# Gate and up: where the residual waits, and a second place for raw weights

## The chip, the cores and the metric

The kernel runs on one core of a Trainium2 chip: TensorE (PE) multiplies, VectorE (DVE), ScalarE (ACT) and GpSimd (POOL) do the work between, SyncE (SP) issues nearly all DMAs. The metric is device time in microseconds, the median of several runs. The profile comes from one further execution.

## The reference, cut to what matters

Two layers act on 1152 tokens (1024 of a prompt, 8 x 16 of samples) with 1024 features. Each layer has a mixer and then a feed-forward part, and the change touches the latter alone:

```python
x = x + mix
x = x + swiglu(rmsnorm(x, p['norm_ffn'][layer]), p['ffn_w_gate'][layer],
               p['ffn_w_up'][layer], p['ffn_w_down'][layer])
```

So silu(h @ w_gate) * (h @ w_up) is formed for 2816 hidden features and multiplied by w_down; all in float32.

## The kernel before, in words

Activations lie as [feature on 128 partitions, tokens on the free axis]. x, the residual, is held in four SBUF tiles x0 to x3 of [128, 2, 1152]: two chunks of 128 features each. A dense product is three float32r matmuls of 384 columns: each operand is split into a rounded part (`whi` for weights) and its remainder (`wlo`), and high x high, high x low and low x high are added in PSUM (`mm3`, L434 to L438).

`ffn` has two stages, gate and up and then down. **Gate and up** runs over 22 tiles of 128 hidden features. For a tile f, SP loads the raw gate weights and the raw up weights, 512 KB each (`raws`, L633). The 24 products of four quarters of the features with three blocks of tokens, for gate and for up, are made of 20 products, as in a fast matrix product: their left operands are sums or differences of quarters of the weights (UP_A, L409), their right operands sums of blocks of activations, which are made once. Each product is 2 chunks x 3 matmuls. The 20 are handled in five panels of four products. For a panel, `weights` (L502)
- forms the sums on POOL (L518) into one of three buffers `cm`. Most sums have 256 columns, and two pairs are done together with 512; two panels have two sums each and take two quarters straight from the raw weights,
- rounds them on ScalarE (L522) into one of three places for split panels,
- takes the remainder on VectorE (L523).

Places and `cm` buffers are passed round. One place and two of the `cm` buffers lie where x2 and x3 were, since x has been turned into the operands by then; so in the trace they are called x, as in "x<-raw" (a sum) or "pa<-u,x" (a matmul). The residual was stored to DRAM (`d_r`) by the stage before.

`tile_of` (L526) orders the products of a tile and the sums of them. ScalarE copies some from PSUM (L549), VectorE adds and subtracts (L555), POOL does one subtraction (also L555), ScalarE applies SiLU (L608), POOL multiplies gate by up (L609), and SP stores the outcome to DRAM (`d_g`, L610), three stores a tile. The room for these is 15 temporaries of 384 columns, handed back after the stores.

The first two tiles are done while the operands are still being made. After them x0 and x1 are free; before the change the residual's first half is loaded there at once (L715 to L717), and tiles 2 to 21 follow in one loop (L724). Their raw weights all go to the same two buffers (L274), one for gate and one for up, so the load for tile f+1 waits until the last panel of tile f has been summed and split. x2 and x3 come back after the loop (L728 to L730), then the down product begins.

Each engine executes its own instructions in one fixed order, which the framework's scheduler sets at build time: by readiness in its own account of the time and by priority, where a priority is the order of the source and `Sooner` moves instructions to the front. Waits are semaphores at the tiles' first and last uses. All loads and stores of this stage go through SP's queue in order.

Of the kernel before, what the change touches and what calls it, by code (L numbers as in the profile page):

```python
"""Hybrid S5 / gated-DeltaNet / sliding-window encoder step on one core.

Activations are held as [feature on partitions, token on the free axis]; the 1024 prompt tokens come
first, then the 8 x 16 sample tokens. A dense product is three float32r passes over operands split
exactly into a rounded part and its remainder."""
# [23 lines left out]
T = TP + NS * LS  # L29
# [15 lines left out]
def ksplit(w):  # L45
    """[K, M] -> [M/128, 128 (k in its chunk), K/128 * 128] panels."""
    k, m = w.shape
    return np.ascontiguousarray(w.reshape(k // 128, 128, m // 128, 128).transpose(2, 1, 0, 3).reshape(m // 128, 128, k))


def halves(w):
    """[1024, 1024] -> [K halves, M/256, 128, 2 * 512] panels."""
    return np.ascontiguousarray(ksplit(w).reshape(4, 2, 128, 2, 512).transpose(3, 0, 2, 1, 4).reshape(2, 4, 128, 1024))


def cols(v):
    """[n * 128] -> [128, n]."""
    return np.ascontiguousarray(v.reshape(-1, 128).T)


def head_order():
    """Column order of q: row halves of a 128-tile hold a head of an even and of an odd kv group."""
    o = []
    for pair in range(2):
        for i in range(4):
            for par in range(2):
                h = 4 * (2 * pair + par) + i
                o += list(range(64 * h, 64 * h + 64))
    return np.array(o)


def s5_order():
    """Order of the S5 channels inside each 128: (channel of a group, group)."""
    return np.arange(512).reshape(4, 8, 16).transpose(0, 2, 1).reshape(512)


def layout(a):
    """The kernel's inputs: moved, copied and zero-padded only."""
# [52 lines left out]
def constants():  # L131
    """Depend on shapes alone."""
# [55 lines left out]
class Chunks:  # L188
    """Chunks of features in tiles of two: x[:, chunk, tokens]."""
# [4 lines left out]
    def new(self, i, shape, dt=F32):  # L194
        """A tile in the place of the i-th."""
# [7 lines left out]
def body(tc, nc, I, O):  # L203
# [19 lines left out]
    def mphase(**tags):  # L223
        """Five banks for the parts between the dense products: one ring, or one for each of the named tiles."""
# [25 lines left out]
    def behind(i, *others):  # L250
        """Queue an instruction behind others of its engine."""
# [4 lines left out]
    def log_tables(*others):  # L256
        """One load of the tables that Ln and Exp share, behind other activations."""
        return behind(S.preload_act_table_set("natural_log_exp_and_others"), *others)

    class Sooner:  # L260
        """Instructions inside go before others that are ready, as if traced n instructions earlier."""
# [16 lines left out]
    def parts(raw, pool=None, bufs=2):  # L278
        """Rounded part and remainder of a panel of weights."""
# [11 lines left out]
    def slots(name):  # L291
        """Per token block, the rounded part and the remainder of 4 + 4 chunks of features."""
# [24 lines left out]
    def sums(sq, w, tag=None):  # L317
        """Sum over partitions of sq, on all partitions (a bank)."""
# [11 lines left out]
    def square_in(x, k, b, i, new, parts, keep=None):  # L330
        """Squares of a chunk into partial sums over chunks; the partial sums with the last chunk.

        One running sum by GpSimd (and one by VectorE), and the last chunk's squares on their own."""
# [15 lines left out]
    def rms(r, b, parts, first=0):  # L349
        """1 / sqrt(mean of squares + eps) of a block's tokens, on all partitions, from parts of the sums of squares."""  # L350
# [18 lines left out]
    def norm(w, h, r, new, first, keep=None):  # L369
        """What fills the scales and, where there are, the operands of a norm as chunk k of block b of x, its i-th, is final."""  # L370
# [24 lines left out]
    # ------------------------------------------------------------------ feed-forward  # L395
    # Gate and up of three blocks of tokens t: with a_0 .. a_3 the gate's and a_4 .. a_7 the up's weights of a quarter q of the
    # features, and b_qt the activations, the 24 products are made of twenty, UP_A[i] times UP_B[i], UP_B in terms of
    # e0 = b_00 + b_01 + b_02 and e1 = b_10 + b_11 + b_12:
    #  0: (a6 - a7) b22                       1: a2 (e1 + b20 + b21 + b30)        2: (a7 - a0) (e0 - b31)
    #  3: -(a2 + a6) (b20 + b22)              4: -(a2 - a3) b30                   5: a0 (b00 + b01 + b12 - b31)  # L400
    #  6: (a6 - a5) b21                       7: (a4 + a7) e0                     8: (a2 - a1) e1
    #  9: -(a0 + a3) b31                     10: -(a4 + a5) b00                  11: -a7 (e0 - b22 - b31 - b32)
    # 12: -(a2 + a5) (e1 + b21)              13: (a5 - a0) (b00 + b12)           14: (a2 + a7) (b22 - b30)
    # 15: a5 (b00 + b11 + b12 + b21)         16: -(a1 + a5) (b10 + b12)          17: -(a0 + a4) (b00 + b02)
    # 18: (a3 + a7) (b30 + b32)              19: -(a0 + a1) b12
    # gate_0 = z + 1 + 4 + 19 - v            gate_1 = v + 5 - z - 8 - 9          gate_2 = 14 + 18 - 4 - 19 - s
    # up_0 = -(0 + 10 + 3 + 14) - z - 1      up_1 = 15 - y - 2 - 5 + 6 + 7       up_2 = y + 0 + 10 + s
    # with z = 12 + 15, v = 13 + 16, y = 13 - P17 and s = 2 + 5 + P11, each number the product of that number.
# [5 lines left out]
    # Down: the first block of tokens is multiplied plainly. For the other two, the four products of halves  # L414
    # C[i][j] = A[i][0] B[0][j] + A[i][1] B[1][j] are made of seven:
    # S1 = A21 + A22, S2 = S1 - A11, S3 = A11 - A21, S4 = A12 - S2,
    # T1 = B12 - B11, T2 = B22 - T1, T3 = B22 - B12, T4 = B21 - T2.
    # Panels of weights give A11 and A12, A21 and A22, S1 and S2, S3 and S4.
    PANELS = (("B11", "B21"), (None, "T4"), ("T1", "T2"), ("T3", "B22"))

    def left(raw, s12):
        """Sums of halves of two raw panels; the last two in place of the first panel, so once that is split."""
# [17 lines left out]
    def reserve(pool):  # L440
        """Place for split panels at the bottom of a pool."""
# [3 lines left out]
    def ffn(x, pre, l, w, nxt):  # L445
# [3 lines left out]
        # gate and up  # L449
# [37 lines left out]
        # sums of weights, split panels, and what the products make  # L487
# [14 lines left out]
        def weights(raw, ps, place=place):  # L502
            """Rounded parts and remainders of the left operands of up to four products."""
# [22 lines left out]
        def tile_of(f, raw, room, order, panels, early=False):  # L526
            """The products of a tile of f: those without the last block of tokens, then the others."""
# [9 lines left out]
            def prods(p, *ps, more=False):  # L537
                """Products into p; more of them, added to what has been read already."""
# [126 lines left out]
        # the first two tiles of f, while the operands of the twenty are made  # L665
# [48 lines left out]
        # x comes back; until then half of its place is for more panels  # L714
        for i in range(2):  # L715
            x.tiles[i] = x.new(i, [128, 2, T])
            Q.dma_start(x.tiles[i], d_r[i])  # L717
        t, u = x.new(2, [128, 2 * T], F32R), x.new(3, [128, 2 * T])
        extra += [[t[:, blk(i, 1024)] for i in range(2)], None, None]
        cms += [u[:, blk(i, 1024)] for i in range(2)]  # L720
        room = rooms[0] + [r[:, blk(UP_T[1])]]
        for t in (some("b13", 1), some(), some()):
            room += [t[:, c] for c in range(2)]
        for f in range(2, NF):  # L724
            last = f == NF - 1
            order = UP_ORDER[16:] + UP_ORDER[:16] if last else UP_ORDER
            finishing(tile_of(f, raws(f), room, order, [(order[i:i + 4],) for i in range(0, 20, 4)], last))
# [6 lines left out]
        # down, by pairs of tiles of f; the products of two pairs go to sums of the seven over all pairs  # L734
# [17 lines left out]
        def load(f):  # L752
            """A tile of f, and room for another block."""
# [12 lines left out]
        def right(ps, last):  # L766
            """Right operands of two pairs, and places for those of the pair that is multiplied plainly."""
# [28 lines left out]
        def into(terms, m, o, first=False):  # L796
            """The products of the terms, tile m of their columns, added to o."""
# [10 lines left out]
        # the last pair is multiplied plainly, and what it gives added with products of the seven that make the same part of x  # L808
        also = {"B21": (0, 1), "T4": (4, 1), "B22": (0, 2)}
        for j in range(0, len(pairs) - 1, 2):  # L810
# [24 lines left out]
            for q in range(4):  # L835
# [5 lines left out]
                for e, n in enumerate(PANELS[q]):  # L841
                    for m in range(4):
# [6 lines left out]
                        if last:  # L849
                            # the sums of the seven make x  # L850
# [26 lines left out]
    # ------------------------------------------------------------------ layer 0  # L877
# [98 lines left out]
    # b and a rows: beta, cumulative log decay and what follows from it  # L976
# [26 lines left out]
    def gate_in(hh, zz):  # L1003
        """The gate of a head."""
# [8 lines left out]
    # S5: u, chunk operators, and the states after each chunk  # L1013
# [11 lines left out]
    # powers 1 to 16 of the step over a chunk  # L1025
# [32 lines left out]
    # prompt: scans inside 8 groups of 16 chunks, then over the groups' ends, then what each group starts with  # L1058
# [27 lines left out]
    # convolutions, and what of the delta rule needs no recurrence  # L1086
# [35 lines left out]
    def l2norms(ys, tables):  # L1122
        """Scale pairs (y, scratch, log of a factor) to unit length of every token."""
# [60 lines left out]
    # inverses of the delta rule's triangular systems' blocks: 32 tokens, one block to a partition  # L1184
# [29 lines left out]
    # S5 outputs  # L1214
# [28 lines left out]
    # v  # L1243
# [25 lines left out]
    # S5: operands of the GLU  # L1269
# [16 lines left out]
    # delta rule, recurrence over 128-token tiles  # L1286
# [13 lines left out]
    def solved(TT, kg, vt, t, uu, wt, tag):  # L1300
        """u and w of a tile from the transposed inverse of its system."""
# [675 lines left out]
```

## Time and profile before

| | |
|---|---|
| median of 3 runs | 2831.28 us (2830.82 to 2835.2) |
| profiled execution: span | 2835.9 us (no other time of it is recorded) |
| TensorE clock granted, mean | 0.953 of full |
| busy: PE, DVE, ACT, POOL | 92%, 70%, 39%, 58% |
| loads of raw gate and up weights | 44 + 44 of 512 KB |
| loads of the residual (x<-d_r) | 8 of 1152 KB |

"Busy" is the share of the span in which an engine had an instruction running; matmuls overlap in the records, so the spacing of their starts tells more than their lengths. An engine's idle time is put down to what ended it, its releaser. In the rows further down a time in brackets is such an idle time.

### The profile page before, as it was taken

How to read it: one execution, taken by the hardware profiler on the slowest of the kernel's cores; microseconds unless marked ns; L12 is line 12 of the kernel's file. 1: busy time of each engine (PE TensorE's matmuls, PEld its weight loads, DVE VectorE, ACT ScalarE, POOL GpSimd, SP SyncE). 2: the span in 40 equal slices, each digit the busy share in tenths (PEclk: the TensorE clock that was granted, in tenths of full speed). 3: DMA queues.
4: the chain of work that ended last, by engine and by line, in shares of the span. 5: the costliest groups of instructions: out<-in, count | busy, mean ns of one | idle time of the engine just before them, and what ended most of it. 6: DMA issues, size and time to landing. Idle time of an engine off the chain costs nothing.

```text
span 2835.9 us, 40158 instructions
## 1 busy us (share of the span) xinstructions
PE 2618.7 (92%) x14777; PEld 2422.3 (85%) x14777; DVE 1977.8 (70%) x3195; ACT 1103.2 (39%) x2232; POOL 1639.5 (58%) x1659
## 2 busy tenths in 40 slices
PE   7898999998799999989999999998799999989996
PEld 6787898897799899989999966668789999979996
DVE  7757855568876666698866245557877666688977
ACT  4233574443433333343333144433333333344332
POOL 8659332225687777788532012114587777788744
PEclk9999999998899999989999999898899999989998
DMA  6523376531122222243213100202022222243311
GB/s 199 155 74 98 107 248 205 180 121 66 56 94 70 70 70 70 70 161 120 91 43 108 59 16 23 89 29 97 32 92 78 75 71 71 70 144 106 110 62 67
DMA packets 164165, 267.20 MB, mean 94 GB/s; under 512 B 34189, under 2 KB 123949, under 8 KB 162929
## 3 DMA queue, kind: packets, MB, share of 16 engines
q1 hardware_dynamic: 163392, 262.28, 28.8%
q8 instruction: 116, 1.90, 0.3%
q10 hardware_dynamic: 576, 2.36, 0.2%
q14 instruction: 81, 0.66, 0.1%
HBM read 186.92 MB, written 79.51 MB: 94 GB/s over the span
## 4 chain that ended last, share of the span: by engine, by line
PE 45%; POOL 22%; DVE 17%; DMA 7%; issue 5%; ACT 3%; SPq 1%; DVEq 0%; ACTq 0%; POOLq 0%
POOL x L518 8%; POOL cm L518 5%; PE pd L436 4%; PE pd L437 4%; PE pd L438 4%; DMA raw<-in_wu_dram 3%; PE pg L307 3%; PE pg L308 3%; PE pg L309 3%; DVE wlo L523 3%; PE pO L1889 2%; DMA raw<-in_wg_dram 2%; PE pg L1514 2%; PE pS L1862 2%; PE pg L1516 2%
## 5 line engine op out<-in xcount | busy, mean ns | idle before, releaser
L518 POOL TENSOR_TENSOR x<-raw 128x256 f32<-128x256 f32 (+1 forms) x372 | 353.1, 976 | 99.0 <-DMA raw<-in_wg_dram 85.5
L436 PE MATMUL pa<-u,whi 128*128 128x384 f32 x928 | 324.8, 350 | 41.4 <-DVE bt L555 14.3
L438 PE MATMUL pa<-u,wlo 128*128 128x384 f32 x928 | 311.2, 345 | 13.7 <-DVE wlo L523 13.7
L437 PE MATMUL pa<-u,whi 128*128 128x384 f32 x928 | 319.2, 344 | 1.7 <-DVE u L469 1.5
L518 POOL TENSOR_TENSOR cm<-raw 128x256 f32<-128x256 f32 (+1 forms) x244 | 236.2, 990 | 78.4 <-DVE wlo L523 28.0
L436 PE MATMUL pd<-g,whi 128*128 128x384 f32 x708 | 240.4, 340 | 0.9 <-DVE bt L555 0.9
L437 PE MATMUL pd<-g,whi 128*128 128x384 f32 x708 | 241.1, 341 | 0.0
L438 PE MATMUL pd<-g,wlo 128*128 128x384 f32 x708 | 238.2, 338 | 0.0
L436 PEld LDWEIGHTS pa<-u,whi 128*128 128x128 f32 x928 | 180.7, 195 | 55.6 <-DVE bt L555 15.9
L523 DVE TENSOR_TENSOR wlo<-x,whi 128x1024 fp32r<-128x1024 f32 (+1 forms) x132 | 155.4, 1177 | 101.7 <-ACT whi L522 101.3
L1850 POOL TENSOR_SCALAR p<-p,rd 128x192 f32<-128x192 f32 (+3 forms) x80 | 59.1, 741 | 287.4 <-DVE rd L1844 175.5
L522 ACT CAST whi<-x 128x1024 fp32r<-128x1024 f32 (+1 forms) x132 | 115.7, 876 | 236.8 <-POOL x L518 209.6
L438 PEld LDWEIGHTS pa<-u,wlo 128*128 128x128 f32 x928 | 179.2, 194 | 17.3 <-DVE wlo L523 17.3
L284 ACT CAST whi<-raw 128x1024 fp32r<-128x1024 f32 x113 | 116.3, 1049 | 178.1 <-PE pg L308 83.0
L437 PEld LDWEIGHTS pa<-u,whi 128*128 128x128 f32 x928 | 180.5, 195 | 3.4 <-DVE u L469 2.3
L436 PE MATMUL pa<-u,x 128*128 128x384 f32 x428 | 150.6, 352 | 31.0 <-ACT x L522 26.8
L285 DVE TENSOR_TENSOR wlo<-raw,whi 128x1024 fp32r<-128x1024 f32 x113 | 162.4, 1438 | 22.3 <-ACT whi L284 22.1
L437 PE MATMUL pa<-u,x 128*128 128x384 f32 x428 | 148.9, 348 | 0.0
L307 PE MATMUL pg<-h0h,whi 128*128 128x384 f32 x384 | 136.6, 356 | 12.4 <-DVE ut L941 11.4
L438 PE MATMUL pa<-u,x 128*128 128x384 f32 x428 | 143.9, 345 | 0.0
L764 DVE TENSOR_TENSOR g<-gf,g 128x384 fp32r<-128x384 f32 x132 | 136.7, 1062 | 5.8 <-ACT g L763 5.8
L436 PEld LDWEIGHTS pd<-g,whi 128*128 128x128 f32 x708 | 133.9, 189 | 1.7 <-DVE bt L555 1.6
(727 smaller groups left out, 7946.2 us busy)
## 6 DMA issues: line engine op xcount, KB each, us to landing
gf<-d_g SPq DMA_DIRECT2D x44, 576.0 KB
raw<-in_wg_dram SPq DMA_DIRECT2D x44, 512.0 KB
raw<-in_wu_dram SPq DMA_DIRECT2D x44, 512.0 KB
raw<-in_wd_dram SPq DMA_DIRECT2D x44, 512.0 KB
raw<-in_win_dram SPq DMA_DIRECT2D x21, 512.0 KB
d_r<-x SPq DMA_DIRECT2D x24, 384.0 KB
x<-d_r SPq DMA_DIRECT2D x8, 1152.0 KB
d_aq<-AQ SPq DMA_DIRECT2D x12, 576.0 KB
```

The source lines that it names most:

```text
L284: S.copy(hi, raw)
L285: V.tensor_sub(lo, raw, hi)
L307: PE.matmul(p[:, :BW], hi[:, c], rh, start=(i == 0), stop=False)
L308: PE.matmul(p[:, :BW], hi[:, c], rl, start=False, stop=False)
L309: PE.matmul(p[:, :BW], lo[:, c], rh, start=False, stop=(i == len(ks) - 1))
L436: PE.matmul(p, hi[:, c], uh, start=start, stop=False, skip_group_check=more)
L437: PE.matmul(p, hi[:, c], ul, start=False, stop=False, skip_group_check=more)
L438: PE.matmul(p, lo[:, c], uh, start=False, stop=stop, skip_group_check=more)
L518: (P.tensor_add if sg > 0 else P.tensor_sub)(cm[:, 256 * j:256 * (j + n)], fa, ga)
L522: S.copy(hi[:, c], src)
L523: V.tensor_sub(lo[:, c], src, hi[:, c])
L764: eng.tensor_sub(op[1], t, op[0])
```

## The change

The two tiles x0 and x1 are no longer filled with the residual after tile 1 of the features. Their room is taken as `back`. Tiles 3, 5, .. 17 load their raw weights into the two halves of the first of them; the even tiles and tiles 19 to 21 use the two buffers as before. When the loop reaches tile 19, the residual's first half is loaded into `back`. The changed file also has its comments and docstrings blanked, with the same line numbers up to the change.

```diff
-        # x comes back; until then half of its place is for more panels
-        for i in range(2):
-            x.tiles[i] = x.new(i, [128, 2, T])
-            Q.dma_start(x.tiles[i], d_r[i])
...
         t, u = x.new(2, [128, 2 * T], F32R), x.new(3, [128, 2 * T])
         extra += [[t[:, blk(i, 1024)] for i in range(2)], None, None]
         cms += [u[:, blk(i, 1024)] for i in range(2)]
+        back = [x.new(k, [128, 2 * T]) for k in range(2)]
         room = rooms[0] + [r[:, blk(UP_T[1])]]
         for t in (some("b13", 1), some(), some()):
             room += [t[:, c] for c in range(2)]
         for f in range(2, NF):
             last = f == NF - 1
+            if f == NF - 3:
+                for i in range(2):
+                    x.tiles[i] = back[i].rearrange("p (k t) -> p k t", k=2)
+                    Q.dma_start(x.tiles[i], d_r[i])
             order = UP_ORDER[16:] + UP_ORDER[:16] if last else UP_ORDER
-            finishing(tile_of(f, raws(f), room, order, [(order[i:i + 4],) for i in range(0, 20, 4)], last))
+            if f % 2 and f < NF - 3:
+                raw = [back[0][:, blk(i, 1024)] for i in range(2)]
+                for n, t in zip("gu", raw):
+                    Q.dma_start(t, I[f"w{n}{l}"][f])
+            else:
+                raw = raws(f)
+            finishing(tile_of(f, raw, room, order, [(order[i:i + 4],) for i in range(0, 20, 4)], last))
         for i in range(2, 4):
             x.tiles[i] = x.new(i, [128, 2, T])
             Q.dma_start(x.tiles[i], d_r[i])
```

## Rows read from the trace of the kernel before

**Rows 1.** The page: the chain that ended last, by engine and by line.
```profile
PE 45%; POOL 22%; DVE 17%; DMA 7%; issue 5%; ACT 3%; SPq 1%; DVEq 0%; ACTq 0%; POOLq 0%
POOL x L518 8%; POOL cm L518 5%; PE pd L436 4%; PE pd L437 4%; PE pd L438 4%; DMA raw<-in_wu_dram 3%; PE pg L307 3%; PE pg L308 3%; PE pg L309 3%; DVE wlo L523 3%; PE pO L1889 2%; DMA raw<-in_wg_dram 2%; PE pg L1514 2%; PE pS L1862 2%; PE pg L1516 2%
```
**Rows 2.** Windows, cut by TensorE's matmuls: tiles 4 to 18, both layers; tiles 6, 7.
```profile
core 0: us, PE busy (x) PEld busy (x) DVE busy (x) ACT busy (x) POOL busy (x), PEclk, DMA share, GB/s
811.20:1162.00 350.80, 326.42 (x1801) 318.79 (x1800) 236.12 (x361) 129.37 (x242) 268.56 (x274) 0.98 0.22 71
2115.60:2466.00 350.40, 327.81 (x1802) 320.05 (x1801) 236.96 (x361) 129.36 (x242) 269.33 (x273) 0.98 0.22 71
855.90:881.80 25.90, 22.81 (x122) 22.49 (x121) 17.13 (x26) 9.51 (x18) 18.75 (x21) 0.93 0.20 64
881.80:903.20 21.40, 21.19 (x122) 20.87 (x121) 14.38 (x23) 8.77 (x15) 17.17 (x19) 1.00 0.24 77
```
**Rows 3.** Timeline, TensorE, tile 6: start, duration, line, operation, idle before.
```profile
858.74 0.33 PE L437 MATMUL pa<-u,whi 128*128 128x384 f32 x1
...
859.95 0.34 PE L438 MATMUL pa<-u,wlo 128*128 128x384 f32 x1
863.38 0.61 PE L436 MATMUL pa<-u,x 128*128 128x384 f32 x1 [3.09 <-ACT x L522]
863.78 0.53 PE L437 MATMUL pa<-u,x 128*128 128x384 f32 x1
...
866.66 0.46 PE L437 MATMUL pa<-u,whi 128*128 128x384 f32 x1
```
**Rows 4.** Waits of TensorE, 844.48 to 1194.54: us, times, longest.
```profile
PE pa L436 <- ACT x L522: 13.4, 5, 3.1
PE pa L436 <- ACT whi L522: 2.2, 2, 1.3
PE b L438 <- DVE wlo L523: 1.7, 3, 0.8
```
**Rows 5.** The chain, 840 to 920: start, duration, what.
```profile
844.48 3.65 DMA raw<-in_wg_dram
...
857.28 0.98 POOL bt L555
...
861.87 0.52 ACT b L608
```
**Rows 6.** POOL's groups, 844.48 to 1194.54: busy, mean ns, idle before, releaser.
```profile
L518 POOL TENSOR_TENSOR x<-raw 128x256 f32<-128x256 f32 (+1 forms) x140 | 131.8, 968 | 36.0 <-DMA raw<-in_wg_dram 31.7 <-DMA raw<-in_wu_dram 4.3
L518 POOL TENSOR_TENSOR cm<-raw 128x256 f32<-128x256 f32 (+1 forms) x70 | 65.4, 956 | 16.4 <-DMA raw<-in_wg_dram 10.5 <-DMA raw<-in_wu_dram 5.9
```
**Rows 7.** Timeline, POOL and VectorE: sums, L555, L609 and a remainder.
```profile
781.25 0.75 POOL L518 TENSOR_TENSOR x<-raw 128x256 f32<-128x256 f32 x1 [4.01 <-DMA raw<-in_wg_dram]
...
848.20 0.73 POOL L518 TENSOR_TENSOR x<-raw 128x256 f32<-128x256 f32 x1 [4.18 <-DMA raw<-in_wg_dram]
...
857.24 1.00 POOL L555 TENSOR_TENSOR bt<-nt,bt 128x384 f32<-128x384 f32 x1
...
859.94 1.15 POOL L609 TENSOR_TENSOR b<-b,bt 128x384 f32<-128x384 f32 x1 [1.69 <-ACT b L608]
860.15 1.22 DVE L523 TENSOR_TENSOR wlo<-raw,whi 128x256 fp32r<-128x256 f32 x1
...
878.85 1.29 POOL L518 TENSOR_TENSOR cm<-raw 128x512 f32<-128x512 f32 x1
```
**Rows 8.** Timeline, SP: the loads of tile 3, of x0, and of tile 6.
```profile
773.64 0.38 SPq L717 DMA_DIRECT2D x<-d_r  x1
775.25 0.33 SPq L275 DMA_DIRECT2D raw<-in_wg_dram  x1
...
777.27 0.33 SPq L275 DMA_DIRECT2D raw<-in_wu_dram  x1
...
844.48 0.36 SPq L275 DMA_DIRECT2D raw<-in_wg_dram  x1
```
**Rows 9.** Line L523, 844.48 to 1194.54: ns shortest/median/longest, first and last start, forms.
```profile
L523 DVE TENSOR_TENSOR wlo<-x,whi x50: 677/1213/1366, 845.2 to 1188.9; 128x1024 fp32r<-128x1024 f32 x30, 128x512 fp32r<-128x512 f32 x20
L523 DVE TENSOR_TENSOR x<-raw,x x20: 411/590/782, 883.2 to 1194.3; 128x256 fp32r<-128x256 f32 x20
```

## The prediction

> **What bounds the kernel now.** First the chain that ended last: 22% of it is POOL, and by line the sums of weights (L518) lead with 8% and 5%, with the loads of raw weights behind them at 3% and 2% [rows 1]. All of these lie in gate and up, so the question is what one tile of features costs there. The windows cut at the first matmul of tiles 4 and 19 hold fifteen tiles each: 350.80 us in layer 0, 350.40 in layer 1, 23.37 a tile [rows 2]. A tile is 20 products of 6 matmuls, 120 matmuls. Undisturbed they start 0.173 us apart (eight starts from 858.74 to 859.95), so TensorE needs 120 x 0.174 = 20.9 us; 2.5 us a tile are lost. Tile 7 took 21.40 and tile 6 before it 25.90 [rows 2]: the loss is uneven, and falls mainly on every third tile.
>
> What it is made of: in tile 6 TensorE stops at 859.95 and goes on at 863.38, then starts matmuls 0.32 us apart from 863.78 to 866.66 (ten starts), which is the 1.2 GHz level; ahead of that it had been idle [rows 3]. So an idle of 3 us costs nearly 1.5 us more at the low clock. In fifteen tiles TensorE waits 13.4 us for casts of ScalarE into the third place for panels (five times, up to 3.1), the largest entry by far [rows 4]. The chain says why that cast was late: 3.65 us of DMA for the gate's weights, then POOL's sums in one burst, POOL's L555 not before 857.28, and VectorE behind it, until ScalarE's SiLU (L608) runs at 861.87; the cast waits behind that SiLU in ScalarE's queue although its sums were ready earlier [rows 5]. At the head stands the load: both buffers of raw weights are in use until POOL has made the last sums of a tile, so SP issues the next gate's weights at 844.48 [rows 8] and the first sum starts at 848.20 [rows 7]. POOL stands idle for these loads 36.0 + 16.4 = 52.4 us in fifteen tiles, 3.5 a tile [rows 6], and is busy 17.9 of the 23.4 (268.56 / 15) [rows 2].
>
> **The change part by part.**
> *Raw weights of tiles 3, 5, .. 17 go into the place of the first quarter of x.* The number of DMAs, sums, casts and matmuls is the same. Tile f+1 no longer shares buffers with tile f for f+1 = 4 to 18: its load waits for the sums of tile f-1 and can be issued a whole tile (21 us) ahead, where 3.7 us are needed. So 15 loads per layer leave POOL's path, 30 in all. The wait that is added (an odd tile's load on the sums of the tile two before) sits on SP; behind it in that queue are only the stores of activations (d_g) and later loads, none of which TensorE waits for within a tile. Those stores free temporaries, of which there are fifteen.
> What it is worth, from both sides. If POOL's 3.5 us fall away and nothing else moves, its tile is 23.4 - 3.5 = 19.9 us, under TensorE's 20.9: so 20.9 is the floor, 2.5 gained. At the other end nothing is gained, because the idle time only moves to another wait. Between: take from TensorE's loss what comes by the late casts: (13.4 us of waits, some 2 more on the casts for the other places, and the low clock after them; five stretches like the 1.5 us of tile 6, about 7.5) = 23 us of 350, 1.5 a tile: 21.9. Or assume that POOL is a tile ahead: only the short waits for VectorE remain, like the 1.7 us for remainders [rows 4], some 0.3 to 0.6 a tile with all of them: 21.2 to 21.5. I take 21.7, nearer to the first, since it counts waits that are in the trace: 1.67 a tile x 30 = 50 us.
>
> *What may hold it back.* Beside TensorE, POOL and VectorE are close to a bound together. A remainder of 256 columns takes VectorE 0.41 us at its shortest [rows 9], but 1.22 at 860.15, while POOL's L609 ran from 859.94 to 861.09: it ended 0.28 after that [rows 7]. So a two-input operation of the one waits for the other. Alone, a tile's POOL work is 12 sums at 0.73, 2 at 1.29 and four further operations at 1.00 (L555 and three L609) = 15.3 [rows 7]; VectorE's remainders are 3 at 1.21, 2 at 0.68, 4 at 0.41 = 6.6 [rows 9]; together 22.0. The Trainium skill ("SBUF — State Buffer", section "SBUF: two separate sides") says that the port pair shared by the two is an exclusive lock held for a whole instruction; the overlap at 860.15 agrees with it. By that rule taken strictly, the shared port alone gives 22.0 a tile, a rival below. But operations in a row start before the one before has ended (back-to-back records overlap by some 0.04 us, and tile 7 ran in 21.40 on TensorE), so 22.0 is too high by up to one, and I keep 21.7.
>
> *The residual.* Its first two tiles (1152 KB each) are no longer loaded at tile 3 but ahead of tile 19. Before, they went out at 773.64 and between the two loads of tile 3's weights (775.25, 777.27) [rows 8], and the first sum came 6.0 us after the issue (781.25), against 3.7 for tile 6 [rows 7]. So tile 3 gains up to 2.3 us a layer. At the new place the load waits for the last sums of tile 17 and so can run during tile 18; if SP puts it right before tile 19's weights, tile 19 pays the same 2.3. I count +2 in all for tile 3 and nothing for tile 19. What needs the residual is the down product, three tiles of 21 us later. Tiles 19 to 21 share two buffers as now and keep their waits.
>
> **Sum.** 50 + 2 = 52 us off. The span of the profiled execution is 2835.9, and no time around it is recorded; it lies 4.6 over the median of the runs (2831.28), 0.16%. 2835.9 - 52 = 2783.9; taken to the median, 2779.
>
> **Rivals.**
> *The shared port binds.* POOL and VectorE's remainders need 22.0 a tile, and POOL is held up besides, as now (23.4 - 17.9 - 3.5 = 2.0 a tile for SiLU and the like) of which perhaps half is port time lost. 22.0 + 0.5 to 1.0 = 22.5 to 23.0: gain 0.4 to 0.9 x 30 = 12 to 27 us: 2804 to 2819. For it: POOL 17.9 and VectorE 15.7 (236.12 / 15) busy of 23.4. Against: tile 7 at 21.40 with the same work.
> *Nothing is gained.* Panels wait for one of three places and three sums buffers; POOL's wait for the load turns into a wait for these, and TensorE's stops stay. 2826 to 2834. For it: TensorE's own wait is on a cast, not on a load [rows 4]. Against: POOL's wait there is put down to the DMA, not to buffers [rows 6].
> *It gets slower.* Each engine takes its work in one fixed order, and weights that are there earlier change that order: sums for the next tile, four of 0.73 = 2.9 us, may be placed on POOL ahead of L555 of the tile before. Then VectorE, ScalarE's SiLU and the cast behind it are late as in tile 6, and TensorE stops for 3 us and runs on at the low clock. Such a tile costs 25.9, another 21.7; today's mean of 23.4 is passed once more than (23.4 - 21.7) / 4.2 = 2 in 5 tiles go that way. With three in five it is 24.2 a tile, + 0.8 x 30 = 25: 2856. Against: earlier loads also let POOL start that burst 3.5 us earlier.
> *More is gained.* TensorE at its floor, 20.9 to 21.2: 66 to 75 us: 2756 to 2765.
>
> **How the numbers follow.** Forecast (21.2 to 22.4 a tile, 2765 to 2801) 0.61, more 0.08, shared port 0.16, nothing 0.08, slower 0.07. The range 2758 to 2814 takes in the forecast, most of "more" and most of the shared port, some 0.8. About 0.2% (5.7 us) is what a measurement of this kernel can tell from no change: faster than that 0.86 (forecast, more, port, and a little of "nothing"), within it 0.07, slower 0.07.
>
> **What would show it.** POOL's idle time ahead of L518 put down to raw weights should fall from 52 us in fifteen tiles to under 5, and in SP's queue the loads of tile f+1 should stand well inside tile f. Both absent: the change doesn't do what it says. TensorE's wait for casts into the third place should fall from 13.4 us to under 4, its granted clock in these windows rise from 0.98 to 0.99 or more, and fifteen tiles take about 325 us. If the load waits go but the windows stay above 338, the shared port shows as longer POOL sums (now 0.96 us a mean [rows 6]); if TensorE's stops multiply behind L608, the order on the queues did it. Tile 19 late behind the residual would show as a first sum 6 us or more after its weights are issued. The forecast is wrong if the windows take over 338 or under 316 us.

## The result and the profile after

The changed kernel takes 2759.08 us (median of 4 runs, 2756.01 to 2761.36), the kernel before 2831.05 (4 runs on the same chip, 2828.52 to 2835.2): ratio 0.974, 95% interval 0.9728 to 0.9751. That is 72 us, where 52 were forecast, and the time of the case "more is gained" (2756 to 2765). The profiled execution took 2758.04 us, its span is 2756.3.

The windows of the kernel after answer to [rows 2]; columns as there. The first two hold tiles 4 to 18 of layers 0 and 1; the other three, gate and up of layer 0, all that lies between, and gate and up of layer 1, each from its first product's matmul.
```profile
core 0: us, PE busy (x) PEld busy (x) DVE busy (x) ACT busy (x) POOL busy (x), PEclk, DMA share, GB/s
805.00:1119.00 314.00, 314.00 (x1801) 314.00 (x1801) 245.28 (x360) 131.83 (x242) 265.01 (x268) 1.00 0.24 80
2073.30:2387.30 314.00, 314.00 (x1801) 314.00 (x1801) 246.93 (x361) 132.26 (x242) 266.80 (x268) 1.00 0.24 80
685.06:1199.40 514.34, 483.63 (x2657) 474.13 (x2656) 406.58 (x567) 210.20 (x385) 419.28 (x408) 0.96 0.25 83
1199.40:1955.70 756.30, 739.97 (x3963) 634.34 (x3963) 475.81 (x987) 274.73 (x741) 274.71 (x236) 0.96 0.21 70
1955.70:2468.70 513.00, 482.49 (x2657) 473.78 (x2655) 409.21 (x569) 210.49 (x385) 421.39 (x408) 0.97 0.25 84
```
Look at the first column against PE's: 314.00 of 314.00, at clock 1.00. Fifteen tiles take 20.93 us each, which is what 120 matmuls take undisturbed; TensorE has no wait left there at all. Before, they took 350.80 and 350.40 [rows 2]: 36.8 and 36.4 less. The whole stage, cut the same way, went from 552.8 to 514.3 and from 550.7 to 513.0, so 73 of the 76 us of the two stages lie in these tiles. Tiles 2 and 3 together give 1.5 in layer 0 and 3.1 in layer 1 (46.5 to 45.0 and 48.2 to 45.1), and tiles 19 to 21 nothing (80.4 to 80.4 and 80.5 to 81.3). The rest of the span, whose source is the same, moved by -4.5, +2.9 and -1.8 us (start, between, end). Together that is the 79.6 by which the profiled spans differ, 7.6 more than the medians. The profiled execution of after lay 1.0 under its median. That of before lay some 6.6 over; this is an estimate, which adds to its span the 1.8 us by which a time exceeds its span in the kernel after.

The page's chain of waits, by engine and by line, against [rows 1]:
```profile
PE 67%; DVE 13%; POOL 11%; issue 3%; DMA 2%; ACT 2%; SPq 0%; DVEq 0%; POOLq 0%; ACTq 0%
PE pa L436 6%; PE pa L437 6%; PE pa L438 6%; PE pg L307 3%; PE pg L309 3%; PE pg L308 3%; PE pd L438 3%; PE pd L436 3%; PE pd L437 3%; PE b L436 3%; PE b L438 3%; PE b L437 3%; PE pO L1897 3%; PE pS L1870 2%; POOL x L518 2%
```
PE went from 45% to 67%, POOL from 22% to 11%, and L518 from the head of the list to its end. The loads of raw weights have left it.

POOL's groups of sums in tiles 4 to 18, the columns of [rows 6]:
```profile
L518 POOL TENSOR_TENSOR x<-raw 128x256 f32<-128x256 f32 (+1 forms) x74 | 66.8, 925 | 8.7 <-DVE wlo L523 5.5 <-DMA raw<-in_wg_dram 3.2
L518 POOL TENSOR_TENSOR x<-x 128x256 f32<-128x256 f32 (+1 forms) x65 | 57.0, 898 | 11.8 <-DVE wlo L523 8.3 <-DMA x<-in_wg_dram 3.5
L518 POOL TENSOR_TENSOR cm<-raw 128x256 f32<-128x256 f32 (+1 forms) x37 | 34.1, 943 | 5.5 <-DVE x L523 5.5
L518 POOL TENSOR_TENSOR cm<-x 128x256 f32<-128x256 f32 (+1 forms) x32 | 29.3, 934 | 6.7 <-DVE x L523 6.2 <-DMA x<-in_wg_dram 0.5
```
The waits for loads fell from 52.4 us to 3.2 + 3.5 + 0.5 = 7.2. What is left on POOL is a wait for VectorE's remainders (L523): a sums buffer is not free yet, because POOL is ahead.

The same turn shows on ScalarE. Its casts' (L522) longest entries of waits (us, times, longest) in these fifteen tiles, first in the kernel before (811.20 to 1162.00), then in the kernel after:
```profile
ACT whi L522 <- POOL x L518: 74.6, 23, 6.1
ACT x L522 <- POOL cm L518: 47.8, 12, 6.0
```
```profile
ACT whi L522 <- PE pa L437: 76.7, 42, 5.2
ACT x L522 <- PE pa L437: 26.6, 27, 2.5
...
ACT whi L522 <- POOL x L518: 6.4, 2, 3.6
```
Before, they waited for POOL's sums. Now they wait for TensorE to give a place for panels back: the line of panels is full from its end, which is what a bound by TensorE looks like from upstream.

The loads in SP's queue, against [rows 8] (the place of x0 goes by x, the shared buffers by raw):
```profile
770.60 0.33 SPq L275 DMA_DIRECT2D raw<-in_wg_dram  x1
771.02 0.38 SPq L727 DMA_DIRECT2D x<-d_r  x1
...
814.55 0.33 SPq L275 DMA_DIRECT2D raw<-in_wg_dram  x1
...
834.29 0.38 SPq L732 DMA_DIRECT2D x<-in_wu_dram  x1
835.04 0.33 SPq L732 DMA_DIRECT2D x<-in_wg_dram  x1
...
1085.52 0.32 SPq L727 DMA_DIRECT2D x<-d_r  x1
```
Tile 6's load stands at 814.55 and its first matmul at 846.8: 32 us ahead, where it was 11.4 before (844.48 to 855.9). Tile 7's stands at 835.04, 33 us ahead. The change was meant to load x0 and x1 of the residual at tile 19, but only x0 goes late (1085.52); x1's place is idle, so its load still goes at 771.02.

### The profile page after: what moved, and what is told of

Same layout as the page of the kernel before. It is cut to its first block, busy times and chain, and to the rows that moved or that the text cites. A ratio compares the mean times of both kernels' runs of the same rounds, so it can differ in the third digit from the quotient of the medians.

```text
span 2756.3 us, 40229 instructions
## 1 busy us (share of the span) xinstructions
PE 2587.2 (94%) x14777; PEld 2404.8 (87%) x14777; DVE 1997.0 (72%) x3195; ACT 1109.8 (40%) x2232; POOL 1643.3 (60%) x1659
## 4 chain that ended last, share of the span: by engine, by line
PE 67%; DVE 13%; POOL 11%; issue 3%; DMA 2%; ACT 2%; SPq 0%; DVEq 0%; POOLq 0%; ACTq 0%
PE pa L436 6%; PE pa L437 6%; PE pa L438 6%; PE pg L307 3%; PE pg L309 3%; PE pg L308 3%; PE pd L438 3%; PE pd L436 3%; PE pd L437 3%; PE b L436 3%; PE b L438 3%; PE b L437 3%; PE pO L1897 3%; PE pS L1870 2%; POOL x L518 2%
## 5 line engine op out<-in xcount | busy, mean ns | idle before, releaser
L436 PE MATMUL pa<-u,whi 128*128 128x384 f32 x928 | 319.6, 344 | 26.5 <-DVE bt L555 13.2
L437 PE MATMUL pa<-u,whi 128*128 128x384 f32 x928 | 317.2, 342 | 1.5 <-DVE u L469 1.2
L523 DVE TENSOR_TENSOR wlo<-x,whi 128x1024 fp32r<-128x1024 f32 (+2 forms) x176 | 202.7, 1170 | 44.9 <-ACT whi L522 44.5
L522 ACT CAST whi<-x 128x1024 fp32r<-128x1024 f32 (+2 forms) x176 | 129.7, 761 | 256.0 <-PE pa L437 148.6
L518 POOL TENSOR_TENSOR x<-raw 128x256 f32<-128x256 f32 (+1 forms) x230 | 209.9, 936 | 25.7 <-DMA raw<-in_wg_dram 14.7
L518 POOL TENSOR_TENSOR cm<-raw 128x256 f32<-128x256 f32 (+1 forms) x162 | 158.9, 1002 | 60.3 <-DVE wlo L523 28.0
L285 DVE TENSOR_TENSOR wlo<-raw,whi 128x1024 fp32r<-128x1024 f32 x113 | 164.6, 1456 | 23.4 <-ACT whi L284 22.7
L436 PE MATMUL pa<-u,x 128*128 128x384 f32 x428 | 146.1, 341 | 4.4 <-DVE bt L555 4.0
L307 PE MATMUL pg<-h0h,whi 128*128 128x384 f32 x384 | 135.0, 352 | 12.1 <-DVE ut L949 11.4
L437 PE MATMUL pa<-u,x 128*128 128x384 f32 x428 | 145.5, 340 | 0.0
L518 POOL TENSOR_TENSOR x<-x 128x256 f32<-128x256 f32 (+1 forms) x142 | 129.2, 930 | 23.1 <-DVE wlo L523 16.4
L438 PE MATMUL pa<-u,x 128*128 128x384 f32 x428 | 141.9, 341 | 0.3
```

The costliest lines, as they stand in the source:

```text
L285: V.tensor_sub(lo, raw, hi)
L307: PE.matmul(p[:, :BW], hi[:, c], rh, start=(i == 0), stop=False)
L436: PE.matmul(p, hi[:, c], uh, start=start, stop=False, skip_group_check=more)
L437: PE.matmul(p, hi[:, c], ul, start=False, stop=False, skip_group_check=more)
L438: PE.matmul(p, lo[:, c], uh, start=False, stop=stop, skip_group_check=more)
L518: (P.tensor_add if sg > 0 else P.tensor_sub)(cm[:, 256 * j:256 * (j + n)], fa, ga)
```

## The experiments

The rival to "POOL's path is the bound and TensorE is next" was first that POOL's work hardly counts, then that the shared port or the length of the load does. Times are set against runs of the kernel before on the same chip; "a tile" is the mean of tiles 4 to 18 of layer 0.

**POOL relieved, loads left alone** (on the kernel before):
```
-                    (V if early else P).tensor_mul(g, g, u)
+                    V.tensor_mul(g, g, u)
```


> The kernel before, with the three products of gate and up a tile (L609) on VectorE instead of POOL; loads and buffers as before. Theory A (a tile takes the longer of TensorE's 20.9 us and of POOL's round, which is its busy time plus its waits; before 17.9 + 3.5 for the load + 2.0 others = 23.4): POOL loses 3 x 1.24 us and the waits for SiLU, its round falls under 20.9 although it still waits for every load, tiles 4 to 18 take 20.9 to 21.4 and the time is 2756 to 2772. Rival B (the load's 3.7 us themselves stall each tile, so only an earlier load helps): 2815 or more. Rival D (POOL and VectorE share a port and this binds): VectorE's 3 x 0.55 take the port in place of 3 x 1.0, some 1.4 us a tile, about 2790.

2795.45 us, ratio 0.9866 (0.9846 to 0.9885): half of the gain, 337.1 / 15 = 22.5 a tile, and a miss for theory A. Moving three operations a tile off POOL (L609, a mean of 1.25 us each) should have sufficed if POOL's busy time alone set the pace. The time is nearest to rival D, the shared port (about 2790), but POOL is busy for only 217.19 of the 337.10 us of tiles 4 to 18, and waits for loads:
```profile
804.50:1141.60 337.10, 323.07 (x1803) 312.01 (x1802) 247.54 (x407) 127.06 (x241) 217.19 (x227) 1.00 0.22 74
```
POOL's longest waits in tiles 7 to 18 of this kernel (us, times, longest):
```profile
POOL x L518 <- DMA raw<-in_wg_dram: 45.8, 8, 7.6
POOL cm L518 <- DMA raw<-in_wg_dram: 22.3, 4, 5.7
```
The end of one round through the buffers, in its timeline:
```profile
899.37 3.51 POOL L518 TENSOR_TENSOR x<-raw 128x256 f32<-128x256 f32 x4 [2.27 <-DVE wlo L523]
...
905.89 0.74 DVE L523 TENSOR_TENSOR x<-raw,x 128x256 fp32r<-128x256 f32 x2
...
906.47 0.33 SPq L275 DMA_DIRECT2D raw<-in_wg_dram  x1
...
910.51 0.73 POOL L518 TENSOR_TENSOR x<-raw 128x256 f32<-128x256 f32 x1 [7.63 <-DMA raw<-in_wg_dram]
```
POOL's last sum ends at 902.9, and the load goes only at 906.47, inside VectorE's remainders of quarters taken straight from raw. The buffers come free with their last reader, which here isn't POOL. POOL has time to spare and spends it waiting for the load, up to 7.63 us at a time.

**The residual's move alone** (on the kernel before):
```
-        for i in range(2):
-            x.tiles[i] = x.new(i, [128, 2, T])
-            Q.dma_start(x.tiles[i], d_r[i])
+        back = [x.new(k, [128, 2 * T]) for k in range(2)]
...
+            if f == NF - 3:
+                for i in range(2):
+                    x.tiles[i] = back[i].rearrange("p (k t) -> p k t", k=2)
+                    Q.dma_start(x.tiles[i], d_r[i])
```

> The kernel before, with the residual's first half asked for at tile 19 and nothing loaded into its place meanwhile. Theory A: only tile 3's weights land earlier, 2824 to 2832. Rival (a good part of the gain is the residual's 2.3 MB gone from tile 3): 2815 or less.

2830.66 us (12 runs), ratio 0.9993 (0.9981 to 1.0004). The time is the one expected, but this run doesn't test the residual's move. Nothing else is loaded into the place, so both loads still go out beside tile 3's weights, as in [rows 8]:
```profile
768.28 0.38 SPq L727 DMA_DIRECT2D x<-d_r  x1
769.88 0.33 SPq L275 DMA_DIRECT2D raw<-in_wg_dram  x1
770.31 0.38 SPq L727 DMA_DIRECT2D x<-d_r  x1
```
Tile 3's first sum starts at 775.78, 5.9 us behind the issue of its weights, where it was 6.0 before. What the residual's move is worth by itself is not shown.

**Second place for half of the tiles** (on the kernel after):
```
-            if f % 2 and f < NF - 3:
+            if f % 2 and f < 11:
```


> The changed kernel, with the second place used for tiles 3, 5, 7 and 9 only, so tiles 4 to 10 have early weights and 11 to 18 don't. Theory A: 7 of 15 tiles at 20.9 us, the others at 23.4, 34 us off: 2790 to 2803. Rival C (the gain comes of another order on the queues, which the build draws up anew, and not of the early loads themselves): no such share; near 2760 or near 2830.

2794.57 us, ratio 0.986 (0.9841 to 0.988). Its windows over tiles 4 to 10 and 11 to 18:
```profile
799.50:946.00 146.50, 146.50 (x841) 146.50 (x841) 112.45 (x165) 61.18 (x111) 124.79 (x125) 1.00 0.24 80
946.00:1133.30 187.30, 173.83 (x962) 170.02 (x961) 125.48 (x194) 68.49 (x129) 140.23 (x145) 0.98 0.22 71
```
146.5 / 7 = 20.93 and 187.3 / 8 = 23.41: in one execution, tiles with the second place run at the floor and those without it at the old pace. POOL's busy time a tile hardly differs (124.79 / 7 = 17.8 us, 140.23 / 8 = 17.5). This is the cleanest evidence that the place for raw weights is what counts, and against another order on the queues as the cause.

**Work added on POOL** (on the kernel after), a product that nothing uses, once a tile, and in a second kernel in each of a tile's three finishes (there without `and t == 1`):
```
                     (V if early else P).tensor_mul(g, g, u)
+                    if not early and t == 1:
+                        P.tensor_mul(u, g, u)
```


> The changed kernel, with one further multiplication of 384 columns a tile on POOL, into a place that is free by then, so its outcome is not used. Theory A: POOL's round is 17.7 + 1.3 + some 2.0 of waits = 21.0, just at TensorE's 20.9: 2757 to 2772. Rival B (with early loads POOL is not a bound at all): 2757 to 2763.

2769.97 us, ratio 0.979 (0.9767 to 0.9813). From tile 6 on the floor holds in layer 0:
```profile
852.10:1124.30 272.20, 272.20 (x1562) 272.20 (x1561) 225.84 (x312) 114.77 (x208) 248.03 (x243) 1.00 0.25 80
```
POOL is busy 91% and costs TensorE nothing there; the time, 11 us longer than that of the kernel after, is lost in tiles 2 to 5 (in layer 1, 2 to 6), 19 and 20.

> The changed kernel, with three further multiplications of 384 columns a tile on POOL, whose outcome is not used. Theory A: POOL's round is 17.7 + 3 x 1.2 to 1.4 + some 2.0 = 23.3 to 23.9, the same as before the change although all loads are early: 2820 to 2850. Rival B: 2770 or less.

2831.79 us (10 runs), ratio 1.0005 (0.9994 to 1.0017): the gain is gone, though POOL waits for loads only 1.9 us in tiles 4 to 18. The windows over tiles 4 to 18, and over the stage of layer 0 and what lies between the two stages:
```profile
810.70:1153.20 342.50, 323.44 (x1802) 312.31 (x1801) 264.34 (x360) 129.66 (x239) 331.57 (x316) 1.00 0.22 73
688.40:1233.80 545.40, 491.40 (x2649) 470.66 (x2648) 425.12 (x563) 206.97 (x383) 497.53 (x467) 0.97 0.23 76
1233.80:1997.90 764.10, 744.65 (x3971) 636.39 (x3970) 482.03 (x992) 275.78 (x744) 281.97 (x240) 0.96 0.21 71
```
POOL is busy 331.57 of 342.50 us and sets 22.83 a tile. TensorE's waits are back, spread over VectorE and ScalarE (us, times, longest):
```profile
PE b L438 <- DVE wlo L523: 2.6, 2, 1.6
PE pa L436 <- ACT whi L522: 2.5, 2, 1.3
...
PE b L436 <- DVE r L555: 2.1, 2, 1.6
PE pa L436 <- DVE bt L555: 1.9, 3, 0.8
```
None names POOL or a load. The short waits for VectorE, which the prediction kept as the part that would remain, appear with a bound upstream and go with it. Some 8 us of this kernel's loss lie between the stages (764.1 against 756.3), where its source is the same as that of the kernel after; why is open.

**The second place for all odd tiles** (on the kernel after), and x0 and x1 of the residual loaded behind the loop instead of at tile 19 (in the trace x1's load still goes out at tile 3, at 774.40):
```
-            if f % 2 and f < NF - 3:
+            if f % 2:
...
```

> The changed kernel, with all odd tiles from 3 to 21 in the second place, and the residual's first half asked for after the loop. Theory A: tiles 19 to 21 no longer wait for their weights, 0.4 and 2.3 us a layer off and a little at tile 21: 2750 to 2756. Rival (the residual comes back too late for the down product): 2760 or more.

2737.59 us, ratio 0.9656 (0.9635 to 0.9678): faster than both kernels, and by more than expected. Tiles 19 and 20 run at 20.9, as thought (21.4 and 23.2 in the kernel after); tile 21, for which only "a little" was counted, falls from 35.7 and 36.9 to 31.4 and 31.5. The two stages take 507.2 and 501.7 us.

**POOL relieved in the kernel after**, and, as a second kernel, in the one with all odd tiles:
```
-                    (V if early else P).tensor_mul(g, g, u)
+                    V.tensor_mul(g, g, u)
```

> The changed kernel, with L609 on VectorE instead of POOL. Theory A: TensorE is at its floor in tiles 4 to 18 already, so nothing there; tiles 2, 3, 19 and 20 may lose some of their waits: 2752 to 2762. Rival (POOL still holds up the kernel elsewhere): 2745 or less.

2748.47 us, ratio 0.9713 (0.9692 to 0.9735), a little more than expected. Tiles 4 to 18 stay at 20.9; the two stages take 509.3 and 508.1, 10 us less, in tiles 0, 1 and 19 to 21.

> Both kernels that beat the changed one put together: all odd tiles from 3 to 21 in the second place, and L609 on VectorE. Tiles 4 to 20 are at TensorE's floor in the one already, so only what L609 on VectorE gave in tiles 0 and 1 is to be had besides: 2728 to 2738. Rival (the two gains are the same): 2737 to 2749.

2736.45 us, ratio 0.9669 (0.9653 to 0.9685). Against the kernel with all odd tiles (0.9656) that is no difference: the two gains don't add.

**A fourth place for split panels in the space of x0** (on the kernel before), with L609 on VectorE and, second, on POOL; the residual's first half is asked for behind the loop:
```
...
-        extra += [[t[:, blk(i, 1024)] for i in range(2)], None, None]
+        extra += [[t[:, blk(i, 1024)] for i in range(2)], [back[0][:, blk(i, 1024)] for i in range(2)], None, None]
...
```


> The kernel before with L609 on VectorE (2795 us as it was run), and the first quarter of x used as a fourth place for split panels rather than for raw weights; the residual's first half is asked for after the loop. All loads of raw weights still go to the two shared buffers. Theory A2 (the load itself is not what costs: with POOL's round short enough, what is left is that a tile's buffers come free only with its last remainder, which waits for a place; one place more gives a panel, 4.2 us, of lead): tiles 4 to 20 near 20.9 to 21.3, time 2735 to 2762. Rival B (the load's 3.7 us stall each tile): 2785 or more.

2819.04 us, ratio 0.9959 (0.9946 to 0.9972): a miss. I had thought that straight quarters were read late for want of a place. POOL still waits for loads, up to 9.6 us, and the load still goes behind the last straight remainder:
```profile
903.29 0.53 ACT L608 ACTIVATE sg<-sg 128x384 f32<-128x384 f32 x1 [2.68 <-DVE sg L555]
903.72 0.70 ACT L522 CAST x<-raw 128x256 fp32r<-128x256 f32 x2
...
905.92 0.42 DVE L523 TENSOR_TENSOR x<-raw,x 128x256 fp32r<-128x256 f32 x1
...
906.41 0.33 SPq L275 DMA_DIRECT2D raw<-in_wg_dram  x1
```
The cast of the straight quarter stands behind a SiLU (L608) that waits 2.68 us for VectorE. So in this round it isn't the place that makes the last reader late but its turn in the queues. Why this kernel (23.1 a tile) is slower than the same with three places (22.5) stays open.

> The kernel before with the fourth place for split panels, L609 on POOL, raw weights in the two shared buffers. Theory A2: POOL's round keeps the wait for the load (17.9 + 3.5 + some 2.0), 23 us a tile, and a fourth place doesn't shorten it: 2800 to 2830. Rival (TensorE was only short of lead, any further buffer cures it): 2775 or less.

2807.13 us, ratio 0.9925 (0.9896 to 0.9954), 22.7 a tile: a place for panels buys about a third of what a place for raw weights does (24 us of 72).

**Every raw load made twice**, the second behind the first (on the kernel before, and on the kernel after; there the loads into the second place too):
```
...
+            for n, t in zip("gu", o):
+                Q.dma_start(t, I[f"w{n}{l}"][f])
...
```


> The kernel before, with every load of raw gate and up weights into the two shared buffers made twice, the second behind the first's landing. Theory L (with one set of buffers a tile's round is load + all sums + last remainder straight from the raw weights, one after the other): each of 40 tiles takes 3 to 4.5 us more, 2940 to 3010. Rival (TensorE has panels in hand, the load is only part of the loss): under 2900.

2928.97 us, ratio 1.0343 (1.0325 to 1.0362): 386.5 / 15 = 25.8 a tile, 2.4 more. Below the range expected, but every tile pays for the longer load.

> The changed kernel with every load of raw gate and up weights made twice, in both places. Theory L (with two sets the load lies beside the other set's sums, and there are some 15 us to spare): tiles 4 to 18 stay at 20.9 us; tiles 19 to 21 share one set and pay 3 to 4.5 each, tiles 2 and 3 some: 2770 to 2800. Rival (loads cost in themselves, by what they move): 2850 or more.

2832.86 us (10 runs), ratio 1.0011 (0.9997 to 1.0024): a miss, 339.1 / 15 = 22.6 a tile. I had taken it that the loads have some 15 us to spare. POOL's timeline in the kernel with doubled loads:
```profile
888.90 3.63 POOL L518 TENSOR_TENSOR x<-x 128x256 f32<-128x256 f32 x4
892.49 1.44 POOL L518 TENSOR_TENSOR x<-raw 128x256 f32<-128x256 f32 x2
...
901.92 0.74 POOL L518 TENSOR_TENSOR x<-x 128x256 f32<-128x256 f32 x1 [5.52 <-DMA x<-in_wg_dram]
```
And in the kernel after:
```profile
840.15 1.33 POOL L518 TENSOR_TENSOR x<-x 128x256 f32<-128x256 f32 x1 [0.35 <-DMA x<-in_wg_dram]
841.44 1.43 POOL L518 TENSOR_TENSOR x<-raw 128x256 f32<-128x256 f32 x2
842.84 1.43 POOL L518 TENSOR_TENSOR x<-x 128x256 f32<-128x256 f32 x2
```
In the kernel after, the weights asked for at 835.04 are summed from 840.15 on, after a wait of 0.35 us: they come just in time. POOL begins the next tile's sums (here from x) among those of the tile before (from raw); in the kernel before it did a tile's sums to the end first. So the lead sits in sums and panels that are made and wait, not in loads that wait. Two loads in a row use that lead up: POOL stalls 5.5 us, and the pace falls from 20.93 to 22.6. Tiles 2, 3 and 19 to 21, which were expected to pay, are 24 us longer in the two layers together.

## Why the prediction was right and wrong

**Right: the mechanism.** POOL's waits for loads left (52.4 to 7.2, "under 5" expected), the loads stand 32 and 33 us ahead of their matmuls, and the clock went to 1.00. With the second place in half of the tiles the gain stops where the place does. It takes both halves of the argument: a place without time on POOL gives little (22.8 a tile with three more operations), time on POOL without a place gives less than half of the tile's gain.

| us a tile | L609 on POOL | L609 on VectorE |
|---|---|---|
| one pair of raw buffers | 23.4 (before) | 22.5 |
| a second pair | 20.93 (after) | 20.93 |

One detail of it was wrong. The prediction has the buffers in use "until POOL has made the last sums of a tile". In the kernel before that holds for 5 of the 14 gate loads of tiles 6 to 19; the other nine, those of the slow tiles among them, go within 0.2 us behind VectorE's last remainder straight from raw. Ahead of the load at 844.48 [rows 8]:
```profile
838.76 4.09 POOL L518 TENSOR_TENSOR x<-raw 128x256 f32<-128x256 f32 x4
842.64 1.67 DVE L523 TENSOR_TENSOR x<-raw,x 128x256 fp32r<-128x256 f32 x2
```
POOL's last sum ends at 842.85, the remainders at 844.31.

**Wrong: the size, in one step.** It is the step "Between", which took 21.7 a tile: 1.67 saved x 30 = 50 us, where 36.8 + 36.4 = 73.2 were. By the prediction's own sign (under 316 us for the fifteen tiles) the forecast failed: they took 314.0. Counting starts of matmuls in tiles 4 to 18 of layer 0 before, TensorE stood 28.7 us (25 distances of more than 0.4 us, each less 0.174) and lost 8.1 at the low clock (63 distances between 0.2 and 0.4), 36.8 in all. The first estimate took off what the trace puts down to casts and the low clock behind them, 23 us; the second let short waits for VectorE remain. Both left a part of TensorE's loss standing without a reason why it should stay. The trace of before puts 7.8 us of TensorE's waits in these tiles down to VectorE; with the line in [rows 4], the longest are (us, times, longest):
```profile
PE b L436 <- DVE bt L555: 1.3, 2, 1.1
PE pa L436 <- DVE b L555: 1.1, 2, 0.6
```
In the kernel after, TensorE has no wait of any kind in these tiles. So the waits belonged to no cause of their own. While the round through the raw buffers (load, sums, last straight remainder, next load) was slower than TensorE, every panel came with little margin, and any engine between could be the last to be late. When the round got faster than TensorE, panels queued up and all of these waits went at once; with POOL made the bound again they came back (the kernel with three more operations). The floor of 20.9 was worked out correctly, and should have been the likeliest value; at 0.08 it stood as a rival.

**The shared port.** It was the largest rival (0.16), and it does not bind here. The two engines do lengthen each other's records, but in all hardly more than before: POOL's L609 went from a mean of 1.25 us to 1.46, its sums of 256 columns from 0.91 to 0.85, VectorE's remainders of 1024 columns from 1.32 to 1.36, and POOL's busy time in fifteen tiles from 268.56 [rows 2] to 265.01. And the records' sum of 22.0 is passed by a measured 20.93. By the distance between starts (0.69 for a sum of 256 columns, from 848.20 [rows 7] to the next at 848.89, and some 0.04 less than its record for each other operation) the sum is about 20.9, by my estimate; with one more operation on POOL it is about 21.8, and the tile still took 20.94 (272.20 / 13). The sum that starts next to the one in [rows 7]:
```profile
848.89 0.74 POOL L518 TENSOR_TENSOR cm<-raw 128x256 f32<-128x256 f32 x1
```
The Trainium skill ("SBUF — State Buffer", section "SBUF: two separate sides") has the port pair as an exclusive lock held for a whole instruction. Added up over the records of a tile, as the prediction did, that gives too much in this case; that one engine's operation lengthens beside the other's, the rows confirm. At POOL's limit the lengthening counts: with three more operations a sum of 512 columns took 1.57 us on average, against 1.29 [rows 7], and a remainder of 1024 columns 1.64.

**The residual** was rated at 2 us, and no run shows that term by itself. The text said that two tiles of it move; one does, since x1's place stays idle and its load is not held. In the kernel after, tile 3's first sum starts at 772.86, 3.9 us behind its load (768.98), and tiles 2 and 3 took 1.5 and 3.1 us less a layer, but there these weights have a place of their own as well. Nothing was late at tile 19 (first sum 3.75 us behind its load), and tiles 19 to 21 kept their waits, as said. **"A whole tile ahead"** was right of TensorE and wrong of POOL, as the doubled loads show.

**What else fell.** "It gets slower" by a changed order: POOL's order did change (sums of the next tile among those of the tile before), and TensorE lost nothing by it. "Nothing is gained" needed the wait to move to places for panels; it did (ScalarE's casts), but with TensorE as the bound such waits cost nothing.

## What to carry to other kernels

Price a second buffer by the round it breaks (load, and the time until its last reader is done, which may not be its main one) against the next bound. Here the round got shorter than that bound, the stage ran at the bound, and all its short waits went too, whichever engine the trace named for them. Then look how far the next engine is from its own limit: here one more operation a tile on POOL was free in the steady tiles, and three cost the whole gain.

## What the runs showed of the hardware

TensorE ran 314 us without a gap, at clock 1.00 and one matmul of 384 columns every 0.174 us, while VectorE was 78% and POOL 84% busy: neither contention nor the clock took anything from it. POOL could be driven to 97% busy, but operations lengthened: a tile with three more had 22.1 us of busy time (331.57 / 15), where the sum is 17.7 + 3 x 1.0 = 20.7 from the kernel after and the undisturbed record of [rows 7].
